# Reordering the queues of a hybrid decoder's mixer stage, with roots as powers on GpSimd and low weight halves made early

## The chip, the cores and the metric

One core of a Trainium2 chip runs the whole program. The time is device microseconds (us) of one execution, less is better. Engines are called by their names in the profile: PE is TensorE (matmuls), DVE is VectorE, ACT is ScalarE, POOL is GpSimd, SP is SyncE, which only issues DMAs.

## The reference, cut to what matters

Two layers; each is a half-step SwiGLU feed-forward block, three mixers side by side that share one input projection `w_in` and one output projection `w_out`, and a second feed-forward block. The sequence has 256 tokens, the model 1024 channels, the feed-forward block 2816.

```python
for l in range(DEPTH):                                   # DEPTH = 2
    x = x + 0.5 * swiglu(rms_norm(x, norm_ffn1[l]), ffn1_w13[l], ffn1_w2[l])
    h = rms_norm(x, norm_mix[l])
    proj = h @ w_in[l]
    z, xbc, dt_raw, cq, ckv, kidx, widx, xl, gl = split(proj)
    y_ssd = ssd_mixer(z, xbc, dt_raw, ...)               # Mamba-2: conv, silu, decays from softplus(dt), norm
    y_att = dsa_mixer(cq, ckv, kidx, widx, ...)          # indexer scores, 64 best keys per query, softmax over them
    y_lru = rglru_mixer(xl, gl, ...)                     # conv, gates, first-order recurrence along the tokens
    x = x + concat([y_ssd, y_att, y_lru]) @ w_out[l]
    x = x + 0.5 * swiglu(rms_norm(x, norm_ffn2[l]), ffn2_w13[l], ffn2_w2[l])
```

`rms_norm` multiplies by the reciprocal root of the mean square plus 1e-6. In `dsa_mixer` it acts on cq, ckv, kidx and on each head of q and k; the index score of a query and a key is a sum over four heads of relu(qi . ki) with weights from widx.

## The kernel before, in words

Every large product is made of three: a weight tile and an activation are each split in two parts, high and low, of the type fp32r, and high x high, high x low and low x high are summed (`mm3`, `mmt`). A raw weight tile comes by DMA into a ring of four buffers (`wraw`); ScalarE copies it to the high half (`whi`, L260), VectorE subtracts to get the low half (`wlo`, L261); each half has four buffers. The helper for this is `wsplit`.

`ffn` walks over 11 blocks of 256 hidden columns, two raw tiles each, then over the second matrix in two halves of 512 output columns. After the last block of ffn1 the norm ahead of the mixers is formed (`norm_block`, `norm_end`).

`mixers` begins with one piece of `w_in` of 460 columns (dt, cq, ckv, kidx, widx): its products go to `pS`, ScalarE scales them by the row norm `nr` into `cs` (L432) and sums squares of cq, ckv and kidx into `lss` (L438). The reciprocal roots `sc` follow (`rsqrt_of`: a first value from the bits of the number, then two Newton steps, ten small VectorE operations). TensorE transposes cq and ckv; q, the index queries and k, v come from small matrices. After rope the index queries and keys are transposed (L506, L508), `scores` multiplies them (L523), ScalarE takes the relu (L526), VectorE sums over the heads (L530). `select` then takes eight maxima at a time off the scores, eight times (MAX, MATCH_REPLACE), on VectorE alone; softmax, the attention output `ya` and the output projection follow.

The decays need softplus of dt: a chain of some two dozen operations of 128 x 16 elements on GpSimd (`softplus`, L155, L156, L191 to L202), which ends in `dt` and `adt` (L638). Three products with `adt` (L641 to L643) give cumulative sums, in `ac`; TensorE spreads each column of `ac` over the partitions (L300) and ScalarE makes the decay tiles M0 and M1 of them (L659 to L664).

The other eight pairs of 128 columns of `w_in` go through `pair`: xl and gl for the recurrence (`lru`, `lru_gate`), B, C and x for the state space mixer (`xbc_pair`, with convolution and silu), and z. `pair` makes two blocks of 24 products of 256 columns each (L251 to L253) with a fresh split for either block.

What is written in which order doesn't fix the queues: a scheduler, run at build time, decides the order of each engine's instructions, and the queues are in order on the chip. `tc.issue_after(ins)` keeps what stands in its block behind `ins`.

Of the kernel before, what the change touches and what calls it, by code (L numbers as in the profile page):

```python
# [31 lines left out]
MAGIC = 1597463007.0  # L32
RS = (64.0 / 9.0) ** 2
# [31 lines left out]
def tile_decoder_trunk(ctx: ExitStack, tc: tile.TileContext, A: dict, out: bass.AP):  # L65
# [79 lines left out]


# [11 lines left out]
    def rsqrt(dst, src, scale, pool, tg, E=V):  # L158

        v = pool.tile(list(dst.shape), F32, name=tg + "v")  # L160
        E.tensor_scalar(v, src, scale * RS, EPS * RS, ALU.mult, ALU.add)
        return rsqrt_of(dst, v, pool, tg, E)

    def rsqrt_of(dst, v, pool, tg, E=V):


        n = list(dst.shape)
        yi = pool.tile(n, I32, name=tg + "y")
        E.tensor_scalar(yi, v.bitcast(I32), -0.5, MAGIC, ALU.mult, ALU.add)
        v2 = pool.tile(n, F32, name=tg + "h")  # L170
        E.tensor_scalar(v2, v, 9.0 / 64.0, None, ALU.mult)
        y = yi.bitcast(F32)
        for i in range(2):
            t = pool.tile(n, F32, name=tg + "t")
            E.tensor_mul(t, y, y)
            E.tensor_mul(t, t, v if i == 0 else v2)
            stt(E, t, t, -10.0 / 3.0, t, ALU.add, ALU.mult)
            z = dst if i == 1 else pool.tile(n, F32, name=tg + "z")
            last = stt(E, z, t, 5.0, y, ALU.add, ALU.mult)
            y = z  # L180
        return last.ins
# [134 lines left out]
    def ffn(n, w13, w2, pool, finish, first=False):  # L316
# [5 lines left out]
        for c in range(KF // 2):  # L322
# [61 lines left out]
    def mixers(n, l, mp, finish):  # L384
# [5 lines left out]
        ya_, yl_ = two("ya_", 1), two("yl_", 1)  # L390

# [42 lines left out]
        lss = mp.tile([P, 3, NH], F32, name="lss", bufs=1)  # L434
        for h in range(NH):
            for i, (o, w) in enumerate(((o_q, 256), (o_kv, 128), (o_ki, 64))):
                sq = mp.tile([P, 256], F32, name="lsq", bufs=1)
                S.activation(sq[:, :w], cs[:, h, o:o + w], AF.Square, accum_out=lss[:, i, h:h + 1])  # L438
        cq, ck = two("cq", 1), one("ck", 1)
        ptq = att_ps()  # L440
        ptk = att_ps()
        for h in range(NH):
            hs = slice(h * P, (h + 1) * P)
            for b in range(2):
                T.transpose(ptq[:, b * SEQ + h * P:b * SEQ + (h + 1) * P], cs[:, h, o_q + b * P:o_q + (b + 1) * P], ident)
            T.transpose(ptk[:, hs], cs[:, h, o_kv:o_kv + P], ident)
# [7 lines left out]
        rsqrt_of(sc, vc, mp, "cr")  # L454
# [8 lines left out]
        qk = mp.tile([P, NH, 8, 64], F32, name="qk", bufs=1)  # L463
# [39 lines left out]
        for h in range(NH):  # L503
            hs = slice(h * P, (h + 1) * P)
            for p_ in range(2):
                T.transpose(pti[:, p_ * SEQ + h * P:p_ * SEQ + (h + 1) * P],  # L506
                            TI[:, h, 2 * p_:2 * p_ + 2].rearrange("p a d -> p (a d)"), ident)
            T.transpose(ptk[:, hs], TI[:, h, 4:6].rearrange("p a d -> p (a d)"), ident)  # L508
# [5 lines left out]
                               ALU.mult, ALU.mult)  # L514

        def scores(qb):
# [3 lines left out]
            for e in range(2):  # L520
                ps = att_ps().rearrange("p (a s) -> p a s", a=2)
                for p_ in range(2):
                    T.matmul(ps[:, p_, :ns], qiT[64 * e:64 * e + 64, p_, qs], kiT[64 * e:64 * e + 64, :ns],  # L523
                             start=True, stop=True)
                rel = two("rel", 2)
                S.activation(rel[:, :, :ns], ps[:, :, :ns], AF.Relu)  # L526
# [34 lines left out]
        rsqrt(qr, qss, 1.0 / 64, mp, "qq", G)  # L561
# [13 lines left out]

        def logits(qb):
# [3 lines left out]
            for e in range(2):  # L580
# [4 lines left out]
                S.copy(pr[:, 2 * e:2 * e + 2], ps[:, :, :ns])  # L585
# [61 lines left out]
        M0, M1 = [], []  # L647
        for g in range(2):
            m0 = mp.tile([P, 4, SEQ], F32, name="m0", bufs=2)
            m1 = mp.tile([P, 4, P], F32, name="m1", bufs=2)  # L650
            for q in range(2):
                pb = mix_ps()
                for i in range(2):
                    hd = 4 * g + 2 * q + i
                    for h in range(NH):
                        bcast_rows(pb[:, i * SEQ + h * P:i * SEQ + (h + 1) * P], ac[:, h, hd:hd + 1])
                for i in range(2):
                    hd = 4 * g + 2 * q + i
                    S.activation(m0[:, 2 * q + i], pb[:, i * SEQ:(i + 1) * SEQ], AF.Relu, scale=-1.0,  # L659
                                 bias=ac[:, 0, hd:hd + 1])  # L660
                    S.activation(m1[:, 2 * q + i], pb[:, i * SEQ + P:(i + 1) * SEQ], AF.Relu, scale=-1.0,
                                 bias=ac[:, 1, hd:hd + 1])
            S.activation(m0, m0, AF.Exp, scale=-1.0)
            S.activation(m1, m1, AF.Exp, scale=-1.0)  # L664
            M0.append(m0)
            M1.append(m1)

# [22 lines left out]
        def xbc_pair(raw, b0, eng, after=None):  # L690
            xr = scaled(pair(raw, 0, eng))
            t = two("xbc", 4)
# [6 lines left out]
        def lru():  # L699
            ps = pair(load_cols(C_XL, 256), 0, (V, V))  # L700
            xr = two("lx", 1)
            conv(xr, scaled(ps), "lru_conv_w", 2, "lru_conv_b", 0)
            la, la2, lt, lb = two("la", 1), two("la2", 1), two("lt", 1), two("lb", 1)
            for b in range(2):
# [5 lines left out]
                for i in range(2):  # L710
                    S.activation(th[:, i], pg[:, i * SEQ:(i + 1) * SEQ], AF.Tanh, scale=0.5, bias=hb[:, i, c:c + 1])
# [12 lines left out]
        def lru_gate(hs):  # L724
            ps = pair(load_cols(C_GL, 256), 0, (V, V))
            gx, hx, gt = two("lx", 1), two("lb", 1), two("lt", 1)
# [8 lines left out]

        hs = lru()


        xbc_pair(load_cols(C_XBC + 512, 256), 4, (V, V), picked)
        xbc_pair(load_cols(C_XBC + 768, 256), 6, (V, V), picked)  # L740

        for g in range(2):
# [4 lines left out]
            cb = mp.tile([P, 3 * P], F32, name="cb", bufs=2)  # L747
# [4 lines left out]
        xbc_pair(load_cols(C_XBC, 256), 0, (V, V))  # L752
        xbc_pair(load_cols(C_XBC + 256, 256), 2, (V, V))

        xdt = []
        for h in range(NH):
# [3 lines left out]
            t = mp.tile([P, 8, 64], F32, name="xdt", bufs=2)  # L760
# [8 lines left out]
        zs, yg = [], []  # L769
        for q in range(2):  # L770
            ps = pair(load_cols(C_Z + 256 * q, 256), 0, (V, V))
            z = two("z", 2)
            V.tensor_mul(z, ps, rb2)  # L773
            silu2(z, z)
            zs.append(z)
        for q in range(2):
            y = two(("la", "la2")[q], 1)
# [11 lines left out]
            yn = two(("lt", "lb")[q], 1)  # L789
# [34 lines left out]
        for q in range(2):  # L824
            sq = two("z", 2)
# [6 lines left out]
        V.tensor_scalar(yv, pss[:, :2 * NH], RS / 256, 4.0 * EPS * RS, ALU.mult, ALU.add)  # L832
        yr = mp.tile([P, 2 * NH], F32, name="yr", bufs=1)
        rsqrt_of(yr, yv, mp, "yq")
# [38 lines left out]
    for l in range(DEPTH):  # L873
        nxt = norm_begin()
        with lined(f"ffn1_{l}") as pool:
# [63 lines left out]
```

## Time and profile before

| | before |
|---|---|
| median of 3 runs | 1023.36 us (1023.26 to 1024.52) |
| profiled execution, own time | 1025.87 us |
| its span, first to last instruction | 1024.1 us |
| mean granted clock of TensorE | 0.988 |
| busy: PE / PEld / DVE / ACT / POOL | 97% / 79% / 65% / 50% / 5% |
| instructions | 12885 |

A busy share is a mean over stages that differ. The granted clock is 1.00 at 2.4 GHz and 0.50 at 1.2 GHz. The mixers of layer 0 lie between 199 and 334 us of the span, those of layer 1 between 705 and 838.

### The profile page before, as it was taken

Reading aid. Unit: us, or ns where it says so; the run is one execution under the profiler, and the core shown is the slowest. Engines: PE = TensorE matmul, PEld = TensorE weight load, DVE = VectorE, ACT = ScalarE, POOL = GpSimd, SP = SyncE. Lnnn points to the kernel's source line nnn. Section 1 sums busy time; section 2 is a strip of 40 time slices with the busy share of each in tenths; the row PEclk is TensorE's granted clock in tenths of the full one; section 3 lists DMA queues with packets and bytes.
Section 4 is the critical chain, followed back from the end, with each engine's and each line's share of the span. In section 5 each row is a group of like instructions: output and inputs, shape, how many; then the busy total and the mean of one; then the engine's idle time right before and its main releaser. Section 6 shows DMA issues by size and latency. Waiting matters only on the chain.

```text
span 1024.1 us, 12885 instructions
## 1 busy us (share of the span) xinstructions
PE 991.1 (97%) x4819; PEld 806.0 (79%) x4819; DVE 661.3 (65%) x1158; ACT 515.2 (50%) x806; POOL 52.7 (5%) x133
## 2 busy tenths in 40 slices
PE   7999999999869999999999999999998999999998
PEld 5888888889844888888888888888897468888886
DVE  6666755576977666664576656555889766566543
ACT  6554545468533554544455445455695255454442
POOL 0600000042000000000000000000500000000000
PEclk9999999999989999999999999999998899999999
DMA  9765555743205565555556555557431256564560
GB/s 318 204 201 175 175 186 167 242 148 109 98 27 184 167 197 177 173 195 194 186 159 207 190 175 176 183 197 229 131 125 42 60 187 206 168 201 149 183 224 21
DMA packets 142752, 172.47 MB, mean 168 GB/s; under 512 B 4851, under 2 KB 114577, under 8 KB 142689
## 3 DMA queue, kind: packets, MB, share of 16 engines
q1 hardware_dynamic: 141792, 171.03, 51.9%
q0 software_dynamic: 864, 0.60, 0.4%
q8 instruction: 38, 0.62, 0.2%
q14 instruction: 26, 0.21, 0.1%
q10 hardware_dynamic: 32, 0.01, 0.0%
HBM read 170.57 MB, written 1.05 MB: 168 GB/s over the span
## 4 chain that ended last, share of the span: by engine, by line
PE 83%; DVE 9%; ACT 3%; DMA 2%; POOL 2%; issue 1%; SPq 0%; ACTq 0%; DVEq 0%; POOLq 0%
PE gu L266 16%; PE gu L268 16%; PE gu L267 16%; PE acc L267 8%; PE acc L268 8%; PE acc L266 8%; PE gu L807 3%; DVE wlo L261 2%; DMA wraw<-in_ffn_w_dram 2%; PE sm L356 2%; DVE xbc L674 1%; PE gu L251 1%; DVE score L542 1%; PE gu L253 1%; PE gu L252 1%; PE sm L289 1%
## 5 line engine op out<-in xcount | busy, mean ns | idle before, releaser
L261 DVE TENSOR_TENSOR wlo<-wraw,whi 128x1024 fp32r<-128x1024 f32 (+1 forms) x304 | 370.5, 1221 | 259.0 <-ACT whi L260 252.7
L260 ACT ACTIVATE whi<-wraw 128x1024 fp32r<-128x1024 f32 (+1 forms) x304 | 321.9, 1061 | 283.5 <-PE gu L268 159.3
L266 PE MATMUL gu<-whi,xh 128*128 128x512 f32 (+1 forms) x736 | 289.8, 396 | 2.5 <-ACT whi L260 2.5
L268 PE MATMUL gu<-whi,xl 128*128 128x512 f32 (+1 forms) x736 | 289.0, 396 | 0.0
L267 PE MATMUL gu<-wlo,xh 128*128 128x512 f32 (+1 forms) x736 | 286.6, 391 | 0.0
L267 PEld LDWEIGHTS gu<-wlo,xh 128*128 128x128 f32 x736 | 138.7, 189 | 28.2 <-DVE wlo L261 0.8
L266 PEld LDWEIGHTS gu<-whi,xh 128*128 128x128 f32 x736 | 138.6, 189 | 28.2 <-ACT whi L260 2.9
L268 PEld LDWEIGHTS gu<-whi,xl 128*128 128x128 f32 x736 | 138.5, 188 | 27.6
L268 PE MATMUL acc<-whi,hl 128*128 128x512 f32 x352 | 137.8, 392 | 0.0
L267 PE MATMUL acc<-wlo,hh 128*128 128x512 f32 x352 | 137.2, 390 | 0.0
L266 PE MATMUL acc<-whi,hh 128*128 128x512 f32 x352 | 135.7, 391 | 0.0
L251 PE MATMUL gu<-xh,whi 128*128 128x256 f32 x256 | 76.3, 298 | 6.3 <-DVE z L773 4.0
L351 ACT ACTIVATE th_s<-gu,rhalf 128x256 f32<-128x256 f32 x88 | 41.8, 475 | 75.9 <-PE gu L268 75.7
L267 PEld LDWEIGHTS acc<-wlo,hh 128*128 128x128 f32 x352 | 66.1, 188 | 13.7
L268 PEld LDWEIGHTS acc<-whi,hl 128*128 128x128 f32 x352 | 66.1, 188 | 13.6
L266 PEld LDWEIGHTS acc<-whi,hh 128*128 128x128 f32 x352 | 66.1, 188 | 13.4
L252 PE MATMUL gu<-xl,whi 128*128 128x256 f32 x256 | 75.4, 295 | 0.0
L253 PE MATMUL gu<-xh,wlo 128*128 128x256 f32 x256 | 75.1, 293 | 0.0
L251 PEld LDWEIGHTS gu<-xh,whi 128*128 128x128 f32 x256 | 50.1, 196 | 8.3 <-issue 5.3
L352 DVE SCALAR_TENSOR_TENSOR th_s<-th_s,gu 128x256 f32<-128x256 f32 x88 | 36.8, 418 | 27.9 <-ACT th_s L351 27.7
L252 PEld LDWEIGHTS gu<-xl,whi 128*128 128x128 f32 x256 | 50.3, 196 | 1.8 <-issue 1.4
L253 PEld LDWEIGHTS gu<-xh,wlo 128*128 128x128 f32 x256 | 50.2, 196 | 1.0 <-issue 0.5
(307 smaller groups left out, 835.1 us busy)
## 6 DMA issues: line engine op xcount, KB each, us to landing
wraw<-in_ffn_w_dram SPq DMA_DIRECT2D x180, 512.0 KB, 4.7
wraw<-in_ffn_w_dram SPq DMA_DIRECT2D x40, 1024.0 KB, 5.0
wraw<-in_w_in_dram SPq DMA_DIRECT2D x16, 1024.0 KB, 5.1
wraw<-in_w_out_dram SPq DMA_DIRECT2D x8, 1024.0 KB, 5.0
wraw<-in_w_in_dram SPq DMA_DIRECT2D x4, 920.0 KB, 4.7
wraw<-in_ffn_w_dram SPq DMA_DIRECT2D x8, 256.0 KB, 5.7
xr<-in_x_dram SPq DMA_DIRECT2D x4, 256.0 KB, 3.9
out_dram<-xr SPq DMA_DIRECT2D x4, 256.0 KB, 2.6
```

Of the source, the lines that this page charges most:

```text
L251: T.matmul(o, lh, rh, start=first, stop=False)
L252: T.matmul(o, lh, rl, start=False, stop=False)
L253: T.matmul(o, ll, rh, start=False, stop=last)
L260: S.activation(hi[sl], raw, AF.Copy)
L261: eng.tensor_sub(lo[sl], raw, hi[sl].bitcast(F32))
L266: T.matmul(o, xh, wh, start=first, stop=False)
L267: T.matmul(o, xh, wl, start=False, stop=False)
L268: T.matmul(o, xl, wh, start=False, stop=last)
L351: S.activation(th, ps[h][:, 0:256], AF.Tanh, scale=rh_[:, h:h + 1])
L352: V.scalar_tensor_tensor(th, th, 1.0, ps[h][:, 0:256], ALU.add, ALU.mult)
L356: T.transpose(pt[:, j * SEQ + h * P:j * SEQ + (h + 1) * P], hf[:, j * P:(j + 1) * P], ident)
L807: T.matmul(acc, y[:, h * P:(h + 1) * P], w, start=t == 0, stop=t == len(ys) - 1)
```

## The change

1. **Roots.** `rsqrt` and `rsqrt_of` become a scaling and one power with exponent -0.5 (`mhalf`), both on GpSimd; the ten VectorE steps (sixteen GpSimd steps for the q and k heads' `qr`) go. It holds for nr, sc, qr and yr.
2. **Early low halves.** For five pairs of `w_in`'s columns (xl, B, C and both of x) the low halves are made in the ffn1 stage ahead, at its blocks 3, 5, 7, 9 and 10: one more load of 1 MB each, two copies on ScalarE, two subtractions on VectorE. They stay in ten tiles `e` of a pool of their own. In the mixers the raw columns are loaded again and only the high half is made. As the tiles come free they hold la, la2, lt, lb, M0, M1, B, C, cb, xdt and z, for which the mixers had tiles before.
3. **Order.** xl's two blocks wait for the transposes of cq and ckv (`turned`); B's second block for the index transposes (`indexed`); C's first block for the first half of the scores of the second 128 queries (`scored[1][0]`); the recurrence's tanh for the relu of their second half (`scored[1][1]`); M0 and M1, now written behind `lru`, for a copy of logits (`copied[1]`).
4. **Squares** of cq, ckv and kidx are written into the tile qk, which is free then, in place of one buffer that all of them shared.

```diff
-    def rsqrt_of(dst, v, pool, tg, E=V):
...
-        yi = pool.tile(n, I32, name=tg + "y")
-        E.tensor_scalar(yi, v.bitcast(I32), -0.5, MAGIC, ALU.mult, ALU.add)
...
-        for i in range(2):
...
+    def rsqrt(dst, src, scale, pool, tg):
+        v = pool.tile(list(dst.shape), F32, name=tg + "v")
+        G.tensor_scalar(v, src, scale, EPS, ALU.mult, ALU.add)
+        return rsqrt_of(dst, v)
+    def rsqrt_of(dst, v):
...
+        return G.tensor_tensor(dst, v, e, op=ALU.pow).ins
...
+    EARLY = [C_XL] + [C_XBC + c for c in (512, 768, 0, 256)]
+    def early_lows(l, ep, i):
+        raw = rp.tile([P, KD, 256], F32, name="wraw")
+        nc.sync.dma_start(raw, A["w_in"][l][:, EARLY[i]:EARLY[i] + 256].rearrange("(k p) c -> p k c", p=P))
+        lows = []
+        for j in range(2):
+            e = ep.tile([P, KD, P], F32R, name="e")
+            r = raw[:, :, j * P:(j + 1) * P]
+            S.activation(e, r, AF.Copy)
+            V.tensor_sub(e, r, e.bitcast(F32))
+            lows.append(e)
+        return lows
...
         for c in range(KF // 2):
...
+            if aside and c in (3, 5, 7, 9, 10):
+                aside(min(c // 2 - 1, 3) if c < 10 else 4)
...
-        def pair(raw, c0, eng):
+        def pair(c0, after=(None, None)):
+            raw = load_cols(c0, 256)
             ps = psg.tile([P, 2, SEQ], F32, name="gu")
             for j in range(2):
-                w = wsplit([P, KD, P], [(slice(None), raw[:, :, c0 + j * P:c0 + (j + 1) * P])], eng[j])
-                block(ps[:, j, :], w)
+                r = raw[:, :, j * P:(j + 1) * P]
+                if c0 in EARLY:
+                    hi = wp.tile([P, KD, P], F32R, name="whi")
+                    S.activation(hi, r, AF.Copy)
+                    w = hi, lows[EARLY.index(c0)][j]
+                else:
+                    w = wsplit([P, KD, P], [(slice(None), r)], V)
+                with behind(after[j]):
+                    block(ps[:, j, :], w)
             return ps
...
-            V.tensor_scalar(vc[:, i], lss[:, i], RS / dim, EPS * RS, ALU.mult, ALU.add)
+            G.tensor_scalar(vc[:, i], lss[:, i], 1.0 / dim, EPS, ALU.mult, ALU.add)
...
-            ps = pair(load_cols(C_XL, 256), 0, (V, V))
+            ps = pair(C_XL, turned)
...
-                    S.activation(th[:, i], pg[:, i * SEQ:(i + 1) * SEQ], AF.Tanh, scale=0.5, bias=hb[:, i, c:c + 1])
+                    with behind(scored[1][1]):
+                        S.activation(th[:, i], pg[:, i * SEQ:(i + 1) * SEQ], AF.Tanh, scale=0.5,
+                                     bias=hb[:, i, c:c + 1])
...
+                    with behind(copied[1]):
+                        S.activation(m0[:, 2 * q + i], pb[:, i * SEQ:(i + 1) * SEQ], AF.Relu, scale=-1.0,
+                                     bias=ac[:, 0, hd:hd + 1])
...
-        xbc_pair(load_cols(C_XBC + 512, 256), 4, (V, V), picked)
-        xbc_pair(load_cols(C_XBC + 768, 256), 6, (V, V), picked)
+        xbc_pair(4, picked, (None, indexed))
+        xbc_pair(6, picked, (scored[1][0], None))
```

How the queues move is seen at three places; rows that differ only in which product of a block they are have been left as they stand.

TensorE's queue in layer 0's mixers before the change, from the products with adt (L641 to L643): behind them stand twelve rows of weight products (L251 to L253), then eight broadcasts of `ac`.

```order
L641 MATMUL acc<-adt,tri 128x8
L642 MATMUL acc<-adt,tri 128x8
L643 MATMUL acc<-adt,ones 128x8
L253 MATMUL gu<-xh,wlo 128x256
L251 MATMUL gu<-xh,whi 128x256
L252 MATMUL gu<-xl,whi 128x256
```

From the broadcasts to the index transposes (L506, L508) and the first scores there are some 30 more such rows; the end of that piece reads:

```order
L252 MATMUL gu<-xl,whi 128x256
L300 MATMUL acc<-ident,ac 128x128 x2
L523 MATMUL sm<-ck,qiT 128x256 x4
L523 MATMUL sm<-ck,qiT 128x128 x2
L300 MATMUL acc<-ident,ac 128x128 x2
```

The same place now: the products with adt (L672 to L674), two products of the recurrence's gates (L720), and at once the index transposes (L532, L534). 

```order
L505 MATMUL sm<-wk,ck 128x512
L672 MATMUL acc<-adt,tri 128x8
L673 MATMUL acc<-adt,tri 128x8
L674 MATMUL acc<-adt,ones 128x8
L720 MATMUL acc<-lx,wbd 128x256 x2
L532 MATMUL sm<-ident,sqc 128x128 x4
L534 MATMUL sm<-ident,sqc 128x128 x2
L242 MATMUL gu<-xh,whi 128x256
```

Then 24 weight products, B's second block, with two more gate products among them, and the scores (L551). The broadcasts of `ac` have moved behind the scores.

ScalarE's queue in layer 0's mixers now, from the eviction of the index keys (L536): the two relus of the first scores (L554) stand ahead of the recurrence's tanh (L725) and exponentials, and M0's relus, which stood ahead of the scores' relus before, far behind.

```order
L536 COPY ck<-sm 128x256
L431 ACTIVATE whi<-wraw 128x1024
L554 ACTIVATE rel<-sm 128x512 x2
L725 ACTIVATE th<-acc,hb 128x256 x4
L728 ACTIVATE e<-th,c_118 128x256
L729 ACTIVATE e<-th,c_118 128x256
L554 ACTIVATE rel<-sm 128x2x128
```

VectorE's queue at the start of layer 0's mixers now: from the norm's last low half (L284) to the first score (L559) there is no weight split (L252) left.

```order
L284 SCALAR_TENSOR_TENSOR xl<-sm,colT_106,xh 128x128 x8
L183 RECIPROCAL spd<-spd 128x16
L475 TENSOR_SCALAR cq<-sm,colT_106 128x256 x2
L476 TENSOR_SCALAR ck<-sm,colT_106 128x256
L511 SCALAR_TENSOR_TENSOR sqc<-cs,sc,kig 128x128 x2
```

The reciprocal of softplus stands ahead of the evictions of cq and ck, and the key's index norm, which reads `sc`, right behind them.

## Rows read from the trace of the kernel before

**Rows 1.** Busy time by stretch: PE, PEld, DVE, ACT, POOL, clock, DMA share, GB/s.

```profile
100.00:150.00 50.00, 50.00 (x229) 40.94 (x228) 32.91 (x63) 23.65 (x30) 0.00 (x0) 1.00 0.51 170
...
199.30:229.90 30.60, 30.57 (x190) 26.33 (x188) 24.15 (x64) 20.52 (x45) 10.58 (x26) 1.00 0.57 181
229.90:246.40 16.50, 15.38 (x116) 15.02 (x117) 8.93 (x17) 11.42 (x26) 7.35 (x22) 0.90 0.39 129
246.40:294.35 47.95, 36.54 (x281) 34.10 (x280) 47.46 (x126) 30.37 (x65) 0.00 (x0) 0.95 0.20 66
294.35:333.90 39.55, 38.67 (x140) 20.54 (x141) 26.63 (x64) 13.00 (x28) 0.00 (x0) 0.97 0.47 147
...
749.50:796.55 47.05, 39.36 (x281) 36.91 (x280) 45.77 (x123) 29.83 (x64) 0.00 (x0) 0.91 0.23 80
```

**Rows 2.** Timeline of PE: start, length, instruction [idle before <- releaser].

```profile
294.35 3.16 PE L807 MATMUL gu<-wraw,ya__1794 128*128 128x512 f32 x4 [0.46 <-ACT ya__1794 L625]
...
796.55 3.78 PE L807 MATMUL gu<-wraw,ya__6119 128*128 128x512 f32 x4 [0.46 <-ACT ya__6119 L625]
```

**Rows 3.** Timeline of DVE: the first sum of scores in each layer.

```profile
246.40 0.48 DVE L530 SCALAR_TENSOR_TENSOR score<-rel,wx,caus 128x256 f32<-128x256 f32 x1
...
749.46 0.48 DVE L530 SCALAR_TENSOR_TENSOR score<-rel,wx,caus 128x256 f32<-128x256 f32 x1
```

**Rows 4.** Timeline of PE, layer 0: products with adt, and the scores.

```profile
231.02 0.39 PE L641 MATMUL acc<-adt,tri 128*128 128x8 f32 x2 [1.15 <-POOL adt L638]
...
242.00 1.57 PE L523 MATMUL sm<-ck,qiT 64*128 64x256 f32 x12
```

**Rows 5.** Timeline of POOL: steps of softplus, the last row from layer 1.

```profile
219.55 1.07 POOL L194 TENSOR_TENSOR sps<-spe,spd 128x16 f32<-128x16 f32 x1 [1.75 <-DVE spd L192]
...
221.00 1.20 POOL L198 TENSOR_SCALAR spc<-spq 128x16 f32<-128x16 f32 x1
...
226.27 0.25 POOL L155 TENSOR_SCALAR stt<-spc 128x16 f32<-128x16 f32 x1
...
228.34 1.42 POOL L155 TENSOR_SCALAR stt<-spc 128x16 f32<-128x16 f32 x1
229.85 0.81 POOL L156 TENSOR_TENSOR dt<-stt,spa 128x16 f32<-128x16 f32 x1
230.74 0.22 POOL L638 TENSOR_TENSOR adt<-dt,a_neg 128x16 f32<-128x16 f32 x1
...
733.92 1.29 POOL L156 TENSOR_TENSOR dt<-stt,spa 128x16 f32<-128x16 f32 x1
```

**Rows 6.** Timeline of DVE: last step of the row norm, layer 0.

```profile
207.38 0.15 DVE L150 SCALAR_TENSOR_TENSOR nr<-nqt,nqz 128x2 f32<-128x2 f32 x1
```

**Rows 7.** Timeline of ACT: first copy to cs, last square, and layer 1's first copy.

```profile
210.52 0.64 ACT L432 ACTIVATE cs<-gu,nr 128x460 f32<-128x460 f32 x1
...
218.09 0.19 ACT L438 ACTIVATION_READ_ACCUMULATOR lsq<-cs 128x1 f32 x1
...
715.93 0.64 ACT L432 ACTIVATE cs<-gu,nr 128x460 f32<-128x460 f32 x1
```

**Rows 8.** Timeline of DVE: low halves beside the long steps of POOL.

```profile
219.39 1.16 DVE L261 TENSOR_TENSOR wlo<-wraw,whi 128x1024 fp32r<-128x1024 f32 x1
...
220.84 1.23 DVE L261 TENSOR_TENSOR wlo<-wraw,whi 128x1024 fp32r<-128x1024 f32 x1
...
228.43 1.22 DVE L261 TENSOR_TENSOR wlo<-wraw,whi 128x1024 fp32r<-128x1024 f32 x1
...
733.91 1.22 DVE L261 TENSOR_TENSOR wlo<-wraw,whi 128x1024 fp32r<-128x1024 f32 x1
```

**Rows 9.** DMA issues: count, KB each, median us from issue to landing.

```profile
wraw<-in_w_in_dram SPq DMA_DIRECT2D x16, 1024.0 KB, 5.1
```

**Rows 10.** Timeline of ACT: the same weight copy in two successive blocks of ffn1.

```profile
621.11 1.05 ACT L260 ACTIVATE whi<-wraw 128x1024 fp32r<-128x1024 f32 x1
...
632.51 1.05 ACT L260 ACTIVATE whi<-wraw 128x1024 fp32r<-128x1024 f32 x1
```

More of the change, by code (lines that the diff above doesn't have):

```diff
@@ L156, in stt @@
         return E.tensor_tensor(out, t, b, op=op1)
-    def rsqrt(dst, src, scale, pool, tg, E=V):
+    def rsqrt(dst, src, scale, pool, tg):
         v = pool.tile(list(dst.shape), F32, name=tg + "v")
-        E.tensor_scalar(v, src, scale * RS, EPS * RS, ALU.mult, ALU.add)
-        return rsqrt_of(dst, v, pool, tg, E)
-    def rsqrt_of(dst, v, pool, tg, E=V):
-        n = list(dst.shape)
-        yi = pool.tile(n, I32, name=tg + "y")
-        E.tensor_scalar(yi, v.bitcast(I32), -0.5, MAGIC, ALU.mult, ALU.add)
-        v2 = pool.tile(n, F32, name=tg + "h")
-        E.tensor_scalar(v2, v, 9.0 / 64.0, None, ALU.mult)
-        y = yi.bitcast(F32)
-        for i in range(2):
[L174 to L181, printed above, removed]
+        G.tensor_scalar(v, src, scale, EPS, ALU.mult, ALU.add)
+        return rsqrt_of(dst, v)
+    def rsqrt_of(dst, v):
+        n = list(dst.shape[1:])
+        names = "abc"[:len(n)]
+        size = 1
+        for k in n:
+            size *= k
+        e = mhalf[:, :size].rearrange(f"p ({' '.join(names)}) -> p {' '.join(names)}", **dict(zip(names, n)))
+        return G.tensor_tensor(dst, v, e, op=ALU.pow).ins
     def softplus(dst, x, pool, tg, E=V):
@@ L381, in ffn, with mixers @@
                         finish(h, c)
-    def mixers(n, l, mp, finish):
+    def mixers(n, l, mp, ep, lows, finish):
         w_in = A["w_in"][l]
@@ L390, in mixers, with halves @@
         ya_, yl_ = two("ya_", 1), two("yl_", 1)
+        def halves(parts=2):
+            t = ep.tile([P, 1024], F32, name="e")
+            n_ = 1024 // parts
+            return [t[:, i * n_:(i + 1) * n_].rearrange("p (a b) -> p a b", a=2) for i in range(parts)]
         def att_ps():
@@ L688, in scaled, with xbc_pair @@
             return xr
-        def xbc_pair(raw, b0, eng, after=None):
-            xr = scaled(pair(raw, 0, eng))
-            t = two("xbc", 4)
+        xbcs = []
+        def xbc_pair(b0, after=None, order=(None, None)):
+            xr = scaled(pair(C_XBC + b0 * P, order))
+            if not xbcs:
+                xbcs.extend(halves())
+            t = xbcs.pop(0)
             with tc.issue_after(after) if after else nullcontext():
@@ L724, in lru_gate @@
         def lru_gate(hs):
-            ps = pair(load_cols(C_GL, 256), 0, (V, V))
-            gx, hx, gt = two("lx", 1), two("lb", 1), two("lt", 1)
+            ps = pair(C_GL)
+            gx, hx, gt = lx, lb, lt
             V.tensor_mul(gx, ps, rb2)
@@ L766, in mixers @@
         lru_gate(hs)
-        zs, yg = [], []
+        zs, yg = halves(), []
         for q in range(2):
[L771 to L775, printed above, removed]
+            ps = pair(C_Z + 256 * q)
+            V.tensor_mul(zs[q], ps, rb2)
+            silu2(zs[q], zs[q])
         for q in range(2):
-            y = two(("la", "la2")[q], 1)
+            y = (la, la2)[q]
             for j in range(2):
@@ L788, in mixers @@
             V.tensor_mul(y, y, zs[q])
-            yn = two(("lt", "lb")[q], 1)
+            yn = (lt, lb)[q]
             for j in range(2):
@@ L824, in mixers @@
         for q in range(2):
-            sq = two("z", 2)
+            sq = zs[q]
             S.activation(sq, yg[q][0], AF.Square)
```

118 lines of the change are left out of this document (65 added, 53 removed).

## The prediction

> **What bounds the kernel now.** I read the table of stretches first, since one average over the whole run hides that two kinds of stage follow each other. In the feed-forward stages TensorE is busy 50.00 of 50.00 us at a granted clock of 1.00 [rows 1]: nothing on another engine can shorten them. The mixers are different. Layer 0's run from 199.3 to 333.9 us and fall into four pieces [rows 1]. To 229.9 TensorE is full (30.57 of 30.60). From there to 246.40, where the first index score is formed, it idles 1.1 us and runs at 0.90. From 246.40 to 294.35, where the output projection begins [rows 2], it idles 11.4 us, at 0.95, while VectorE is busy 47.46 of 47.95: there top-64 and softmax set the pace. Then the projection, 38.67 of 39.55 us, is TensorE's again. So the time of a mixer stage is set by when the first score reaches VectorE, plus some 48 us that VectorE fills, plus the projection. Layer 1 repeats this (first score 749.46, projection 796.55 [rows 2, 3]; the same piece 749.50 to 796.55 has 7.7 us of idle TensorE and a clock of 0.91 [rows 1]).
>
> What makes the first score late is seen by following it back: the scores' matmuls run at 242.00 and the cumulative sums of adt at 231.02, which waited on POOL [rows 4]. POOL worked on softplus, one small step after another, until 230.96 [rows 5], and although the scores need none of it, TensorE's queue is in order, so adt's three products hold back all that stands behind them.
>
> **The change part by part.** Layer 0 is worked out; layer 1 is read off it.
>
> *The order of the start.* The row norm nr came at 207.38+0.15 on VectorE, after ten steps with weight splits between them [rows 6]. Now it is two POOL steps behind nsum. The first cs copy was at 210.52 and the last square ended at 218.28 [rows 7], with VectorE's low halves and TensorE's recurrence blocks between. Some twelve recurrence products (0.12 each, 1.4 us) no longer stand among those of cs, so I place the first copy at 209.1. From it to the last square was 7.8 us with four weight copies on ScalarE between; two are left, at 1.05 [rows 10] each, so 5.7: 214.8. That is 3.5 us earlier.
>
> *POOL's chain.* Before: sps starts at 219.55, adt ends at 230.74 + 0.22 = 230.96, so 11.4 us. In it single steps of the same shape take 0.22 to 0.25 us at one time and 0.81 to 1.43 at another [rows 5]. The long ones lie beside a VectorE low half: sps beside 219.39, spc beside 220.84, a stt beside 228.43 [rows 5, 8]. In layer 1 it is another instruction that is long, dt at 733.92, and again a low half is at 733.91 [rows 5, 8]. So the length is not the step's own. Less the excess of four long steps (0.85 + 0.95 + 1.17 + 0.59 = 3.6) the chain takes 7.9 us. The early low halves take ten weight splits of 1.22 us [rows 8] from VectorE here per layer, and no split is left ahead of the first score, so I take 7.9. Ahead of sps POOL now has three scalings (0.9), spd (0.3), a power x, spa (0.3). Sum: 214.8 + 1.5 + x + 7.9, and 0.2 for seams: adt at 224.4 + x.
>
> The Trainium skill ("SBUF — State Buffer", section "SBUF: two separate sides") says that VectorE and GpSimd share one port pair as an exclusive lock, and that a VectorE operation with two SBUF inputs makes a GpSimd operation that reads SBUF wait for its whole length. The trace agrees in both layers with the rows just named; by the rule the chain shortens, and if it were wrong the chain would stay at 11.4, which is the first rival below.
>
> *What a power costs.* The trace holds none. Nearest rows: a POOL step of 16 elements, 0.22 to 0.25 us unblocked, 1.43 blocked [rows 5]. A power could be worth several simple steps, so the bounds are 0.2 and 3; I take 0.5, nearer to the plain rows. It replaces ten small VectorE steps (sixteen on POOL for qr), so a cut in VectorE's queue of about 1.5 us per norm (ten of 0.15 [rows 6]) comes with it; I count it nowhere else. adt: 224.9 against 230.96, 6.0 earlier.
>
> *From adt to the score.* Before, adt to score was 231.0 to 246.40, 15.4 us: between them stand a whole weight pair and fourteen broadcasts in TensorE's queue. Now adt (0.7), two gates (0.9) and the index transposes (0.7) come one behind the other, and 24 products of 0.12 with two more gates (3.7) cover the eviction of qi and ki; then scores 0.9, and 0.7 for the first relu. The products are estimates from their spacing in the trace (256 columns 0.12; adt's first two 0.39 [rows 4]). TensorE reaches adt at about 225, so it doesn't wait. Score at 224.9 + 0.7 + 0.9 + 0.7 + 3.7 + 0.9 + 0.7 = 232.5. That is 13.9 earlier than 246.40. In layer 1, whose same point is 749.46 and whose stage lies 715.93 - 210.52 = 505.4 later [rows 7], 11.5.
>
> *From score to projection.* VectorE was full there, so it must carry its 47.5 us again. It gains one weight split (1.13 apart) and one scaled block (0.6) that stood ahead of the score, and loses two z splits and conv steps now elsewhere (2.0); waits between MAX and MATCH that no split fills any more cost about 1. So 48.3: projection at 280.8, 13.5 earlier; 10.3 in layer 1.
>
> *TensorE's cap.* The work displaced behind the score must fit under the same 48 us. TensorE's idle time up to the projection is 0.03 + 1.1 + 11.4 us, and its clock loses 0.10 of 16.5 and 0.05 of 47.95, 4.0 us: 16.6 in all, and some 12 in layer 1. A gain of 13.5 would leave only 3 idle, with both engines near full and their queues in order, ScalarE at two thirds beside them. I take off 1.5 per layer: 12 and 9.
>
> *The early low halves.* Five loads of 1024 KB per layer, ten copies and ten subtractions in the feed-forward stages, where VectorE is busy 32.91 of 50 and ScalarE 23.65 [rows 1]: hidden, at nothing, but for one place. The fifth is issued behind the ninth block's raw load, and both engines treat it before that block's own split. A 1 MB load takes 5.1 us [rows 9]; two copies (2.1), a low half (1.2) and the block's own low half (1.2) make 9.7 us after a raw slot frees. A block takes 632.51 - 621.11 = 11.4 us [rows 10], and three of four whi tiles ahead of TensorE are worth 8.6. Short by 1 us in each layer; bounds 0 and 3 (the clock may drop after a wait).
>
> *The others* (squares written to qk, reuse of the e tiles, M0 behind the logits' copies) go at nothing: M0's relus and exponentials now lie in the 48 us, where ScalarE is busy 30.37 [rows 1]; if it were late with them, VectorE's products of M0 and cb would wait, by up to 2 us.
>
> **Sum.** 12 + 9 less 2 x 1 = 19. The profiled execution takes 1025.87 (its span 1024.1 and 1.8 around it), so 1006.9; it is 2.5 above the median of 1023.36, which gives **1004.4**.
>
> **The rivals.**
> 1. *The chain is only partly freed* (0.25). The long POOL steps are their own price, or the queues, now in a fixed order, wait for each other: XL's and the gates' copies for the scores, TensorE for a late weight half. For it: TensorE would be nearly full. Against: the pattern of long steps moves between layers. 3.6 us back per layer gives 1011; with 3 more per layer for queue waits, 1017.
> 2. *Slower: the power is slow on POOL* (0.07). In each mixer sc's power stands ahead of softplus and qr's ahead of the first score on VectorE, where 3 us are covered: the score moves by 2x - 3. Against the sum's 19 it decides from x = 6.3 on (two layers of 9.6); at x = 8 it costs 2 x 13 - 19 = 7 more than now: 1030. Nothing in the trace shows an elementwise step beyond 1.43 on 16 elements.
> 3. *TensorE's idle time goes altogether* (0.13). Then the cap holds: 28 us, and with the projection's own loss up to 32: 991 to 995. For it, the work moved behind the score is about 14 us, just the size of the gaps.
> 4. *The change does nothing to the score* (0.03): if VectorE still gets the first score at 246 because qr or the index norm on POOL ends last, about 1023.
>
> **How the numbers follow.** The forecast has 0.52 with its own range 999 to 1009. With rival 3 as far as 992 and rival 1 to 1017 the range holds about 8 in 10. A measurement can tell 0.2%, 2 us, from no change. Faster: 0.52 + 0.25 + 0.13 = 0.90. Same 0.03, slower 0.07.
>
> **What would show it.** Right: the first score some 14 us earlier against the start of the mixers; POOL's steps from sps to adt within 9 us and none above 0.5; powers under 1 us; the score-to-projection piece still 48 us long with VectorE full and TensorE above 45 busy; ten splits fewer in a mixer stage; one short TensorE wait behind the fifth early load. Wrong: powers of several us; that piece longer by what the score gained (TensorE or ScalarE had become its bound); long POOL steps with no VectorE step beside them; or feed-forward stages that lengthen by more than 3 us.

## The result and the profile after

| | before | after |
|---|---|---|
| median | 1023.94 us (1023.26 to 1026.76, 4 runs timed beside those of the changed kernel) | 1000.8 us (1000.49 to 1001.15, 4 runs) |
| span of the profiled execution | 1024.1 us | 999.2 us |
| TensorE busy in it / not busy | 991.1 / 33.0 us | 981.4 / 17.8 us |
| mean granted clock | 0.988 | 0.999 |

The changed kernel is faster: 0.977 of the time before, 95% interval 0.975 to 0.9788. TensorE runs the same 4819 products in both, so the gain splits into two terms: of 24.9 us of the span, 15.2 come from time in which it stood idle, and 9.7 from the same products taking less time, at a mean granted clock of 0.999 in place of 0.988.

The table of stretches of the changed kernel, with the same columns as before: PE, PEld, DVE, ACT, POOL busy, clock, DMA share, GB/s. The first four rows are layer 0; they end where adt is ready on POOL, at the first score, at the start of the output projection and at the next stage. The last row is layer 1, from its first score to its projection.

```profile
199.30:223.70 24.40, 24.40 (x145) 20.80 (x144) 12.59 (x33) 16.16 (x40) 9.95 (x33) 1.00 0.72 226
223.70:232.65 8.95, 8.95 (x64) 7.88 (x63) 4.99 (x11) 4.48 (x9) 4.86 (x7) 1.00 0.00 1
232.65:281.15 48.50, 46.55 (x380) 44.99 (x380) 47.46 (x123) 39.68 (x86) 0.02 (x1) 1.00 0.33 109
281.15:320.50 39.35, 37.21 (x137) 19.66 (x138) 26.46 (x51) 13.36 (x28) 1.92 (x3) 1.00 0.47 143
...
725.15:773.65 48.50, 46.55 (x380) 45.00 (x379) 47.45 (x123) 39.68 (x86) 0.03 (x1) 1.00 0.33 109
```

Against [rows 1]: the clock is 1.00 in all these rows, TensorE idles 1.95 us between score and projection where it had idled 11.4, and both layers are now alike to the hundredth. VectorE's 47.46 us there are as many as before, but TensorE's 46.55 are nearly as many now: it runs 380 products there in place of 281.

The first score on VectorE and the start of the projection on TensorE, in both layers (timeline of DVE, then of PE), which answer to [rows 3] and [rows 2]:

```profile
232.65 0.49 DVE L559 SCALAR_TENSOR_TENSOR score<-rel,wx,caus 128x256 f32<-128x256 f32 x1
...
725.16 0.48 DVE L559 SCALAR_TENSOR_TENSOR score<-rel,wx,caus 128x256 f32<-128x256 f32 x1
```

```profile
281.15 1.98 PE L848 MATMUL gu<-wraw,ya__1811 128*128 128x512 f32 x4 [0.46 <-ACT ya__1811 L656]
...
773.65 1.98 PE L848 MATMUL gu<-wraw,ya__6045 128*128 128x512 f32 x4 [0.46 <-ACT ya__6045 L656]
```

In layer 0 the score is 13.75 us earlier, the projection 13.2. The projection's first four products take 1.98 us; in layer 1 before they took 3.78 [rows 2], at half clock, after a wait of 2.92 us for the attention output.

POOL's timeline in layer 0, the powers and the ends of the softplus chain, against [rows 5]:

```profile
202.45 0.73 POOL L172 TENSOR_TENSOR nr<-nqv,mhalf 128x2 f32<-128x2 f32 x1
...
214.43 1.36 POOL L172 TENSOR_TENSOR sc<-vc,mhalf 128x6 f32<-128x6 f32 x1
...
215.97 0.23 POOL L185 TENSOR_TENSOR sps<-spe,spd 128x16 f32<-128x16 f32 x1
...
223.47 0.22 POOL L669 TENSOR_TENSOR adt<-dt,a_neg 128x16 f32<-128x16 f32 x1
...
228.62 2.93 POOL L172 TENSOR_TENSOR qr<-qqv,mhalf 128x16 f32<-128x16 f32 x1
```

From the start of sps to the end of adt are 7.7 us in place of 11.4, with no step above 0.42 between. The time of a power grows with the elements in each partition: 0.73 us for 2, 1.03 for 4 (yr), 1.36 for 6, 2.93 for 16.

### The profile page after: what moved, and what is told of

The parts are those of the page before. It is cut to its first block, busy times and chain, and to the rows that moved or that the text cites. A ratio compares the mean times of both kernels' runs of the same rounds, so it can differ in the third digit from the quotient of the medians.

```text
span 999.2 us, 12815 instructions
## 1 busy us (share of the span) xinstructions
PE 981.4 (98%) x4819; PEld 800.1 (80%) x4819; DVE 649.3 (65%) x1046; ACT 532.0 (53%) x826; POOL 53.0 (5%) x130
## 4 chain that ended last, share of the span: by engine, by line
PE 85%; DVE 7%; DMA 3%; ACT 3%; issue 1%; SPq 0%; ACTq 0%; DVEq 0%
PE gu L258 16%; PE gu L257 16%; PE gu L259 16%; PE acc L259 8%; PE acc L258 8%; PE acc L257 8%; PE gu L848 3%; DMA wraw<-in_ffn_w_dram 2%; PE sm L364 2%; DVE e L684 1%; DVE wlo L252 1%; PE gu L242 1%; PE gu L243 1%; PE gu L244 1%; PE sm L280 1%
## 5 line engine op out<-in xcount | busy, mean ns | idle before, releaser
L252 DVE TENSOR_TENSOR wlo<-wraw,whi 128x1024 fp32r<-128x1024 f32 (+1 forms) x284 | 345.7, 1220 | 224.0 <-ACT whi L251 216.7
L251 ACT ACTIVATE whi<-wraw 128x1024 fp32r<-128x1024 f32 (+1 forms) x284 | 299.1, 1057 | 250.9 <-PE gu L259 135.2
L259 PEld LDWEIGHTS acc<-whi,hl 128*128 128x128 f32 x352 | 66.1, 188 | 13.5
L242 PE MATMUL gu<-xh,whi 128*128 128x256 f32 x256 | 73.8, 288 | 1.6 <-DVE cx L697 1.6
L244 PE MATMUL gu<-xh,e 128*128 128x256 f32 x160 | 46.8, 293 | 0.0
L362 DVE TENSOR_TENSOR hf<-th_s,gu 128x256 f32<-128x256 f32 x88 | 36.9, 421 | 2.9
```

The costliest lines, as they stand in the source:

```text
L242: T.matmul(o, lh, rh, start=first, stop=False)
L244: T.matmul(o, ll, rh, start=False, stop=last)
L251: S.activation(hi[sl], raw, AF.Copy)
L252: eng.tensor_sub(lo[sl], raw, hi[sl].bitcast(F32))
L259: T.matmul(o, xl, wh, start=False, stop=last)
L362: V.tensor_mul(hf, th, ps[h][:, 256:512])
```

## The experiments

Twelve kernels, each timed beside the kernel before on the same chip. The kernel before had medians from 1023.53 to 1025.85 there, so that a difference of 2 us between two kernels of different sets is not resolved. "Lows" are the early low halves, "powers" the roots as powers, "order" the five constraints. All keep the small rest of the change (M0 written behind the recurrence, squares in qk); no kernel has this rest alone, so what it is worth is not shown, but together with the order it wins nothing (x4). Idle and busy are TensorE's over the profiled span, the score is layer 0's first one. The profiled execution of x3 is its fastest, 1006.68.

| kernel | lows | powers | order | median us | ratio to before (95%) | idle / busy us | score at |
|---|---|---|---|---|---|---|---|
| changed | yes | yes | yes | 1000.8 | 0.975 to 0.9788 | 17.8 / 981.4 | 232.65 |
| x1 | no | yes | yes | 1014.43 | 0.9884 to 0.9924 | 25.6 / 988.5 | 237.72 |
| x2 | yes | no | yes | 1008.32 | 0.9815 to 0.9862 | 22.1 / 986.2 | 233.64 |
| x3 | yes | yes | no | 1009.19 | 0.9826 to 0.9868 | 19.7 / 985.2 | 234.75 |
| x4 | no | no | yes | 1026.09 | 1.0002 to 1.0023 | 32.9 / 990.2 | 241.52 |
| x9 | yes | no | no | 1009.3 | 0.9829 to 0.9861 | 23.8 / 985.9 | 234.97 |
| x10 | no | yes | no | 1014.87 | 0.9888 to 0.9917 | 27.0 / 986.1 | 238.73 |

### Without the early low halves

```diff
-    EARLY = [C_XL] + [C_XBC + c for c in (512, 768, 0, 256)]
+    EARLY = []
...
```

The argument of `ffn` that makes the early loads goes as well.

> No low halves are made in ffn1; powers and order stay. My theory (the gain is an earlier first score, and both VectorE's missing weight splits and the order make it early): seven splits stand again on VectorE ahead of the first score, POOL's steps beside them take over 0.8 us again, softplus from sps to adt is back from 7.7 to 10 or 11 us, the first score comes 4 to 7 us later, and the 48 us behind it carry a split or two more: 1010 to 1016. Rival A (early low halves are all of it): 1020 or more. Rival B (the order is all of it): 1000 to 1003, with POOL's steps short.

The time is 1014.43, in my theory's range. Steps of POOL are long again, and for the reason it gave. Timeline of POOL, then of DVE, of this run:

```profile
221.58 1.24 POOL L182 TENSOR_SCALAR spd<-spe 128x16 f32<-128x16 f32 x1
...
224.14 1.06 POOL L185 TENSOR_TENSOR sps<-spe,spd 128x16 f32<-128x16 f32 x1 [1.11 <-DVE spd L183]
```

```profile
220.34 2.35 DVE L252 TENSOR_TENSOR wlo<-wraw,whi 128x1024 fp32r<-128x1024 f32 x2
...
223.97 1.16 DVE L252 TENSOR_TENSOR wlo<-wraw,whi 128x1024 fp32r<-128x1024 f32 x1
```

The steps that are long are now spd and sps, which take 0.27 and 0.23 in the changed kernel; each ends with the low half beside it (222.82 and 222.69; 225.20 and 225.13). So the length comes from VectorE. The Trainium skill ("SBUF — State Buffer", section "SBUF: two separate sides") says that the two engines share a port pair, and that a VectorE operation with two SBUF inputs and a GpSimd operation that reads SBUF block each other: the one that starts later waits. The trace agrees. But it is the smaller part, and smaller than I expected: from sps on, the chain takes 8.5 us against 7.7, where I had 10 or 11. The score is 5 us late chiefly because POOL gets to its scalings of the squares only at 219.42, 6 us later than in the changed kernel. Behind the score, the 48.5 us become 53.5 in layer 0: VectorE's work grows to 51.22 there, and TensorE's clock is 0.94.

```profile
237.72:291.25 53.53, 49.92 (x379) 47.85 (x377) 51.22 (x129) 40.02 (x85) 0.19 (x1) 0.94 0.30 99
```

Which of the two makes the piece longer was not taken apart. In layer 1 neither happens (46.71 us of VectorE, clock 1.00) and the piece takes 49.04: layer 0 loses 10.1 us up to its projection, layer 1 only 3.8.

### Without the powers

The edit takes back the Newton steps (`rsqrt`, `rsqrt_of` and their callers).

> The roots are Newton steps again (VectorE, for qr POOL); early low halves and order stay. My theory: with no splits between them the ten steps of nr and of sc take about 2 us instead of 5, against 0.7 and 1.4 us of the powers; qr's sixteen steps take 4.5 us against 2.9 of its power; TensorE's cover takes part of it: the first score 1 to 3 us later, 1002 to 1006. Rival C (the powers carry the gain, as POOL and VectorE no longer hand over): 1010 or more.

The time is 1008.32, between my range and rival C. The score is only 1.0 us late, as I had it. The rest is lost behind it: the piece up to the projection takes 50.63 us with 46.80 of TensorE, and then the clock falls. Windows of this run, up to the projection and of its first 7.7 us:

```profile
233.64:284.27 50.63, 46.80 (x381) 45.11 (x380) 48.19 (x125) 39.72 (x86) 1.23 (x3) 0.98 0.32 105
...
284.27:292.00 7.73, 7.73 (x18) 3.73 (x19) 3.08 (x6) 1.08 (x2) 0.00 (x0) 0.66 0.00 0
```

TensorE had waited 2.48 us for the attention output; behind that wait the granted clock is 0.66 over 7.7 us, where the changed kernel, which waits 0.69 there, has 1.00 over the same first 8 us. The clock takes 0.34 of 7.73, 2.6 us; in layer 1, behind a wait of 2.47 us, it takes 0.21 of 8.0, 1.7 us. So a wait of some 2.5 us at that place costs its own length and 1.7 to 2.6 us more.

### Without the order, and order alone

x3 drops all five constraints; x4 keeps them and drops the two other parts.

```diff
-            ps = pair(C_XL, turned)
+            ps = pair(C_XL)
...
-                    with behind(scored[1][1]):
+                    with behind(None):
...
-                    with behind(copied[1]):
+                    with behind(None):
...
-        xbc_pair(4, picked, (None, indexed))
-        xbc_pair(6, picked, (scored[1][0], None))
+        xbc_pair(4, picked)
+        xbc_pair(6, picked)
```

> None of the five order constraints; powers and early low halves stay, M0 still written behind the recurrence. My theory: TensorE reaches the index transposes 16 products later by its order, about the same time; ScalarE has two tanh and three exponentials ahead of the scores' relu, 2 to 3 us: the first score 2 to 4 us later, 1004 to 1009. Rival A: no more than 1 us from the changed kernel, 1000 to 1002. Rival B (the order is all of it): 1018 or more.

> Only the order constraints (and M0 behind the recurrence, squares in qk): Newton roots, no early low halves. My theory: the first score is 5 to 9 us later than in the changed kernel, with long POOL steps and eight splits ahead of it, 1011 to 1019; less than the kernel before, since fourteen broadcasts and M0's relus have left the scores' way. Rival B: 1000 to 1004. Rival A: 1022 to 1024, as before.

x3, at 1009.19, is just above my range (its four runs lie from 1006.68 to 1009.76). x4 refutes me: order alone gives nothing, which was rival A's condition. Yet its first score came as I had it, 8.9 us later than in the changed kernel and 4.9 earlier than in the kernel before. So an earlier score is not by itself an earlier end. TensorE's longest wait (total, times, longest) and the stretch of layer 0 from the score to the projection say why:

```profile
PE acc L684 <- POOL adt L681: 11.4, 2, 5.7
```

```profile
241.52:294.32 52.80, 49.06 (x377) 47.25 (x375) 49.43 (x126) 39.21 (x85) 0.00 (x0) 0.94 0.30 101
```

The constraints clear TensorE's queue of other work and leave it standing before the products with adt, which POOL gives at 231.0 as it did before. The work so moved stands behind the score: 377 products there in place of 281 [rows 1], for which TensorE needs 49.06 us at a clock of 0.94. From 199.3 to the projection TensorE idles 9.8 us in place of 12.6, but is busy 85.3 in place of 82.5, at a clock of 0.93 in place of 0.96: what it wins by idling less it loses by the clock. So the projection starts at 294.32, where it started before the change (294.35).

### Order alone, with adt out of the way

```diff
+        with behind(scored[1][0]):
-        T.matmul(pac[:, 0:8], tri, adt[:, 0], start=True, stop=True)
+            T.matmul(pac[:, 0:8], tri, adt[:, 0], start=True, stop=True)
```

> Order alone (1026) once more, with one more constraint: the products with adt wait for the first scores. Order alone left TensorE waiting 5.7 us per layer for adt, with the index transposes behind it. My theory (the order only pays if nothing late stands at the head of TensorE's queue): that wait goes, the first score moves from 241.5 to 236 or earlier, the time falls by 6 to 10: 1016 to 1020. Rival G (without early low halves VectorE and POOL hold the score anyway, qr being ready at 237): 1023 to 1026.

The time is 1022.0 (0.9968 to 0.9998 of before), 2 us above my range and 1 below rival G's. The score is at 239.79, where I had 236 or earlier, which speaks for G. The wait goes to the next late thing, with the same length:

```profile
PE sm L544 <- DVE sqc L534: 11.8, 2, 5.9
```

sqc needs sc, whose Newton steps stand on VectorE between weight splits and end at 230.3; in the changed kernel sc is there at 215.8. The score is 6.6 us earlier than before the change, and once more the piece behind it is longer (54.14 us), so that the projection starts at 293.93, 0.4 us earlier. So order pays where lows and powers have made both adt and sc early. The table says the same: order wins 8 us with both; with lows alone (x9 to x2) the difference is 1.0 us, with powers alone (x10 to x1) 0.4, and neither is resolved.

### Lows alone, powers alone

These are x2 and x1 without the five constraints.

> Only the early low halves (and M0 behind the recurrence, squares in qk): Newton roots, no order constraints. If the parts add up, as the runs without one part say (without early low halves 14 us lost, without powers 8, without order 8, of 23), early low halves alone win 14 less the overlap: 1009 to 1013. Rival F (the parts only work together, as order and nothing else won nothing): 1018 or more.

> Only the powers (and M0 behind the recurrence, squares in qk): no early low halves, no order constraints. If the parts add up: 1014 to 1017. Rival F (the parts only work together): 1021 to 1026. POOL's steps beside weight splits stay long in either case.

The times are 1009.3 and 1014.87, both in the ranges for parts that add up. They win 16.6 and 11.0 us against 1025.85, the median of the kernel before beside them, and rival F falls for these two. But both together without order (x3) win no more than lows alone, so adding up fails as well: powers and order are worth 8 us together on top of the lows, and each alone 1 us or less, which is not resolved. Whether the powers win by taking ten steps out of VectorE's queue or by being short was not taken apart.

### Does the chain still pace the changed kernel?

x5 puts three powers that nothing reads ahead of sc; x11 makes sc wait for three of them (`zero` is a tile of zeros):

```diff
+        for i in range(3):
+            v1 = mp.tile([P, 3, NH], F32, name="late", bufs=1)
+            G.tensor_tensor(v1, vc, zero[:, :6].rearrange("p (a b) -> p a b", a=3), op=ALU.pow)
+            v2 = mp.tile([P, 3, NH], F32, name="vc2", bufs=2)
+            G.tensor_mul(v2, vc, v1)
+            vc = v2
         rsqrt_of(sc, vc)
```

> Three more powers of six elements, of 1.36 us each, on POOL ahead of the one that gives sc; nothing reads them. My theory (in the changed kernel the chain over POOL to the first score still has next to no slack: adt was there 1.15 us before TensorE came to it, qr 0.2 us before VectorE would have taken the score): adt 4.1 us later, TensorE waits about 3 us, the first score 3 to 4 us later, and the stage ends as much later: 1006 to 1010, TensorE's new idle time standing before adt. Rival D (TensorE is full now and the chain has slack behind it): within 2 us of the changed kernel, 1000 to 1003.

> The changed kernel with sc truly later: three powers with exponent 0 (1.36 us each) and three multiplications by their result (0.22 each) in a chain ahead of sc, 4.7 us; nothing else changes in what is computed. In the run with three free powers the build moved adt's products behind the scores and the time stayed. My first theory (the way to the first score has no slack): the first score 4 us later, 1007 to 1010. Rival D (adt is off the way when TensorE's order allows, VectorE has slack between sc and the index transposes, and TensorE has been full ever since): the first score at most 2 us later and the time 999 to 1003.

The times are 999.34 and 999.55: no slower than the changed kernel, and my theory fell twice. In x11 sc starts at 221.51, 7 us later than in the changed kernel, adt at 228.31, 4.8 later; the build answered by putting adt's products behind the scores, and the first score came earlier, at 230.59. Timeline of PE, then of DVE, in x11, and its stretch behind the score:

```profile
228.80 1.57 PE L559 MATMUL sm<-ck,qiT 64*128 64x256 f32 x12
230.30 0.39 PE L680 MATMUL acc<-adt,tri 128*128 128x8 f32 x2
```

```profile
230.59 0.48 DVE L567 SCALAR_TENSOR_TENSOR score<-rel,wx,caus 128x256 f32<-128x256 f32 x1 [1.00 <-ACT rel L562]
```

```profile
231.00:281.00 50.00, 48.91 (x391) 47.07 (x391) 47.50 (x125) 39.60 (x86) 2.92 (x3) 1.00 0.31 106
```

A score 2 us earlier moved the projection by only 0.5 (280.64): VectorE has 2.5 us to spare in this stretch and TensorE 1.1, so there TensorE is the nearer to its limit. In the changed kernel the two are within a microsecond of each other (47.46 and 46.55 of 48.50). Where adt may stand behind the scores, adt has at least 4.8 us of slack and sc 7.

### Which of the five constraints

x7 drops the three on TensorE's blocks and keeps ScalarE's two; x8 the other way round.

> The changed kernel without the three constraints on TensorE's blocks (xl, B, C); ScalarE's two (tanh, M0's relus) stay. All five free cost 8 us. My theory: TensorE's queue moves little (16 products), the loss is ScalarE's queue: 1000 to 1003 here. Rival H (TensorE's order is what counts): 1006 to 1009.

> The changed kernel without the two constraints on ScalarE (tanh behind the scores' relu, M0's relus behind the logits' copies); TensorE's three stay. My theory: tanh, exponentials and four of M0's relus stand ahead of the scores' relu, the first score comes 3 us later: 1006 to 1010. Rival H: 1000 to 1003.

x8, at 1010.27, is just above my range: the first relu comes at 234.74 in place of 232.02, and the score at 235.40. x7, at 1018.67, is worse than dropping all five (1009.19), which neither theory had. Waits of TensorE in x7, and its stretch behind the start of the projection:

```profile
PE sm L654 <- DVE ya L650: 6.4, 2, 3.2
```

```profile
287.99:296.00 8.01, 8.01 (x19) 3.91 (x20) 3.12 (x6) 0.47 (x1) 0.00 (x0) 0.72 0.00 1
```

It pays for a wait of 3.2 us per layer for the attention output, which x3 does not have, and for the half clock behind it. Why VectorE gives the attention output so late there (the piece up to the projection takes 52.09 us, 50.01 in x3) was not taken apart. So the five work as a set: ScalarE's two alone are worse than none, and TensorE's three alone are no better.

### A version that is faster still

The changed kernel's longest new wait stands inside the projection, as the waits of TensorE list it (before, the same wait was 1.9 in all, 1.0 at most):

```profile
PE gu L848 <- DVE xr L853: 3.4, 2, 2.1
```

VectorE's sums of the projection stand behind a weight split for ffn2, whose raw tile comes late. One more constraint lets the sums go first (`summed` collects the scaled sums of the projection; its fourth is handed to ffn2 as `held`):

```diff
-                with tc.issue_after(n.last) if c == 1 else nullcontext():
+                with (tc.issue_after(n.last) if c == 1 else tc.issue_after(held) if held is not None and c == 0 and q == 1
+                      else nullcontext()):
```

> The changed kernel with one more order constraint: the low halves of ffn2's second raw tile wait for the fourth scaled sum of the output projection, so that VectorE's sums no longer stand behind a split whose weights come late. My theory: TensorE's waits for these sums, 2.1 and 1.3 us, fall below 0.5 in both layers and nothing else moves: 997 to 999. Rival E (ffn2's first block then gets its weight halves late): the wait moves into ffn2, 1000 to 1002.

The time is 997.48 us (997.09 to 997.5, 4 runs), 0.9712 to 0.9741 of before: 3.3 us faster than the changed kernel, with intervals that don't meet. The wait is gone from the list, and only one of 0.8 us came in; TensorE idles 15.8 us in place of 17.8, 6.8 of them in two waits of 3.4 each, for the first parameters and for a first weight half. The span is 3.4 us shorter; the other 1.4 are busy time of TensorE (980.0 us for 981.4).

## Why the prediction was right, point by point

- **Direction and size.** 1004.4 was forecast, 1000.8 came; 19 us against 23.1 by the medians and 24.9 in the profiled spans, 5.9 more than the sum. Three terms make this up: the deduction for queues (2.2 in both layers), the loss in ffn1 (2), and 2.0 behind layer 1's projection that the sum did not have; 0.3 is lost again between the layers.
- **The mechanism.** In the changed kernel it came as named: adt came early, the score came early, and some 48 us stood behind it. But the rule that it was drawn from, that the first score sets a mixer stage's time, since VectorE fills the 48 us behind it, does not hold by itself: in x4 and x12 the score came 4.9 and 6.6 us earlier than before and the projection 0.0 and 0.4, and in x11 a score 2 us earlier brought 0.5. What the runs fit is the account that the prediction kept as TensorE's cap. From 199.3 to layer 0's projection TensorE runs 584 to 591 products in all fourteen kernels, and in the changed one they take 79.9 us at a clock of 1.00. What comes on top is lost: before, 12.6 us by idling and 2.6 by the clock; now 1.95 by idling.
- **The start and POOL's chain.** Last square 214.8 forecast, 213.8 measured; chain from sps 7.9 forecast, 7.7 measured; adt 224.9 forecast, 223.7 measured. The powers were mis-sized: 0.5 taken, 1.36 for sc and 2.93 for qr, inside the bounds of 0.2 and 3, but not the "powers under 1 us" named as a sign of being right. It was luck that this did not show: POOL's scalings ran in part before the last square had ended, and from that square's end to sps it took 2.2 us all the same, as forecast. x1 shows the long steps to be VectorE's doing.
- **From adt to the score.** 232.5 forecast, 232.65 measured, since TensorE came to adt at 224.84, where 225 was forecast. That adt itself was 1.2 us earlier than forecast won nothing. And the step that lets the score follow adt failed in the changed kernel: there is slack, since x11 delays sc by 7 us and adt by 4.8 for nothing.
- **From score to projection.** 48.3 forecast, 48.5 measured; 13.5 forecast, 13.2 measured. The 1.5 us per layer taken off for queues that wait for each other was the first term mis-sized: it is 0.3 in either layer. The step "with both engines near full and their queues in order" failed, since the constraints put the right work ahead: 1.95 us of idle TensorE were left. In x2, x3 and x7, without the powers or with fewer constraints, TensorE idles 3.8, 3.4 and 6.5 us in this piece.
- **The early low halves in ffn1.** Short by 1 us per layer behind the fifth load was forecast, the second term mis-sized: TensorE does not wait there in either layer. The run has one wait for a low half of ffn1, 0.2 us at 522.62, and that is behind the first load of layer 1. The rows are the fifth load of layer 0 in the changed kernel (median us to landing), ScalarE's copies of it, and that one wait.

```profile
wraw<-in_w_in_dram SPq DMA_DIRECT2D x1, 1024.0 KB, 6.8
```

```profile
107.05 2.01 ACT L317 ACTIVATE e<-wraw 128x1024 fp32r<-128x1024 f32 x2 [2.07 <-DMA wraw<-in_w_in_dram]
```

```profile
PE gu L258 <- DVE wlo L252: 0.2, 1, 0.2
```

  The load took 6.8 us, longer than the 5.1 I took; it went out at 100.2, the end of the low half of 98.95, and the block's own next low half ended at 111.71, 11.5 us after that where I had 9.7. TensorE still did not wait. The step that failed is "three of four whi tiles ahead of TensorE are worth 8.6", counted from the freed slot: after it two more low halves, at 103.29 and 105.22, were made from a raw tile that was already there, and they added to the stock.

- **Layer 1.** Its own gain up to the projection was forecast as 10.3 less the deduction; measured are 10.0. Its projection starts 22.9 us earlier (796.55 to 773.65), and 12.9 of these are layer 0's (505.4 us between the layers before, 492.5 now). Another 2.0 us, of 24.9 in the profile, come behind the projection's start; the clock over its first 8 us was 0.66 before and is 1.00 now.
- **The rivals.** The first (long steps are POOL's own price) falls by x1. The second, a slow power, was no danger to sc: even 7 us more ahead of it cost nothing (x11), as the build reordered. A slower power for qr was not tried. The third came nearest: of TensorE's 33.0 us of idle time 17.8 were left in the whole run, and of the 11.4 in layer 0's widest gap 1.95. The fourth falls with the score at 232.65.

## What to carry to other kernels

Where an engine with an in-order queue waits for one late result, reordering alone left it to wait for that one or for the next late one (x4, x12); first make the late results early, by taking the work away from the engines that hold them up, then order the queues. A milestone that comes earlier is not yet a gain: count what the fullest engine still loses, by idling and by its clock, up to the end of the stage. After the change, ask again what binds: here TensorE is nearly full, and a chain that stood on the way before has slack to spare. For a bound engine read the waits of that engine alone, and with each the granted clock behind it, which here nearly doubled the price of some waits and left others as they were.

## What the hardware showed that I had not expected

The time of a power on POOL grows with the elements per partition, from 0.73 us for 2 to 2.93 for 16, an estimated 0.16 us each beyond a base of some 0.4 (worked out from those two), while a multiplication of 16 takes 0.22. With exponent 0 (x11) six elements take 1.35 to 1.37 us, with -0.5 1.36.

The clock makes short waits dear, but the length of the wait alone doesn't tell the price. The projection's first four products took 1.98 us after a wait of 0.69 for the attention output, 3.78 after 2.92 (layer 1 before), but 3.16 after 5.07 (layer 0 before). The changed kernel's wait of 2.14 us inside the projection left the clock at 1.00. And one and the same wait, 1.08 us for the attention output in layer 0, was followed by a clock of 1.00 over the next 3 us in x9 and of 0.63 in x10, though TensorE had been busy 4.19 of 5.26 and 4.25 of 5.33 us up to its end, at 1.00 in both:

```profile
283.26 0.44 PE L666 MATMUL sm<-ident,ya 128*128 128x128 f32 x2 [1.08 <-DVE ya L662]
...
286.33 0.44 PE L654 MATMUL sm<-ident,ya 128*128 128x128 f32 x2 [1.08 <-DVE ya L650]
```

What makes the difference no run here shows.
